# Triangular inverses of two linear-attention heads on 32-row diagonal blocks, with 32-column matmuls and block transposes on the vector engine

## The chip, the cores and the metric

One core of one Trainium2 chip runs the whole kernel in one launch. The metric is the device time in microseconds (us), the median of several executions. The kernel is written with a scheduling layer: the program is written in one order, and the layer lays down a fixed order of instructions for each engine, by data dependences, by free buffers and by priority (work written earlier goes first unless a `first()` block lifts it). Each engine then works through its own list in order.

## What is computed

The reference is three transformer blocks, one after the other, on 512 tokens of 1024 channels in float32. The change touches the second block alone, whose two mixers run on chunks of 128 tokens and need the inverse of a unit lower triangular matrix for each head and chunk:

```python
def chunk_gated_delta_rule(q, k, v, g, beta):        # "gdn" in the kernel
    ...
    lower = jnp.where(strict, jnp.einsum('bhncd,bhnsd->bhncs', k_beta, k) * decay, 0.0)
    t_mat = lax.linalg.triangular_solve(lower + eye, ..., left_side=True, lower=True, unit_diagonal=True)
    u = jnp.matmul(t_mat, v_beta)
    ...
def rwkv7_scan(r, decay, k, v, a, b):                # "rwkv" in the kernel, done chunk by chunk there
    def step(S, inp):
        sa = jnp.einsum('bhvk,bhk->bhv', S, a_t)
        S = S * w_t[...] + sa[..., None] * b_t[...] + v_t[..., None] * k_t[...]
        return S, jnp.einsum('bhvk,bhk->bhv', S, r_t)
```

Both mixers have 8 heads of 64 channels. A 128x128 inverse is needed for 4 chunks x 8 heads in each.

## The kernel before

Weights stream in pieces of eight 128x128 blocks (`load`, L318): a DMA, a copy to a high part on ACT (L325) and a subtraction for the low part on DVE (L326). A projection of 128 output columns (`lin`) is, for each of 8 weight blocks, three matmuls of 512 columns (L364, L365, L366): 24 in all. They are called weight matmuls below. Their results lie in three PSUM banks named `mm` and are read there by ACT and DVE.

The second block's mixers are in `second` (L1142). It runs over four columns of heads, j = 0 to 3, two heads a column. For each j, `rwkv` (L1297) and `gdn` (L1450) are generators that `run` steps in turn, so that their instructions are written alternately. Then come the projections for the next column (`lins(j + 1)`: seven of 24 weight matmuls) and one or two projections for gates (`aside`; twelve after the last column). Being written later, they have lower priority, and the scheduling layer puts their weight matmuls wherever it holds TensorE (PE) to be free. Tiles of `rwkv` have names with `ra` and PSUM banks `r` (3), those of `gdn` `ga` and `g` (2).

Each of the two calls `invert` (L677) once a head, so 4 inverses a column and 16 in all; one call does the four chunks together, in tiles of 128x512 (`Lt`: the strictly triangular matrices; `Tt`: the inverse, transposed; `Ti`: the inverse). The two inverses of a mixer are stepped in turn. The method doubles the size of inverted diagonal blocks: from blocks of b rows to 2b, the off-diagonal part is minus a product of inverse, triangular matrix and inverse.

- Start: two DVE operations on 128x512 (L684, L685), four PE transposes into PSUM and one ACT copy out (L652 and L656, by `transposes`).
- Five levels, b = 2, 4, 8, 16, 32. Each: an ACT copy that gathers the odd blocks of `Lt` (L700); a product of two 128x128 matmuls with 128 columns (L704); a mask on DVE out of PSUM (L708, 128x256); a second such product (L711); a subtraction on DVE (L713, 128x256); and, so that `Tt` follows `Ti`, an ACT copy that gathers (L692), two PE transposes and an ACT copy out of PSUM (`turned`, by L652 and L656). After b = 32 there are four transposes instead.
- End, from 64 to 128: four 64x64 matmuls (L724), DVE (L727), four more (L731), DVE (L733).

All are float32, and a float32 matmul stands in the trace as two records, a transpose as one.

Of the kernel before, what the change touches and what calls it, by code (L numbers as in the profile page):

```python
# [11 lines left out]
AF = mybir.ActivationFunctionType  # L12
ALU = mybir.AluOpType
# [4 lines left out]
P = 128  # L18
# [43 lines left out]
def prep(i, only=(1, 2, 3)):  # L62
# [85 lines left out]
    c.add("m1", ((r[None] % 2 == 1) & (r[:, None] == r[None] - 1)).astype(f))  # L148
    g = np.arange(64)
    for b in (2, 4, 8, 16, 32):  # L150
        c.add(f"lev{b}", (r[:, None] // b == r[None] // b).astype(f))
# [422 lines left out]
class Chain:  # L574
# [102 lines left out]
    def invert(self, Lt, out):  # L677

        z, V, A, T = self.z, self.z.V, self.z.A, self.z.T
        quad = lambda x: x.rearrange("p (u n) -> p u n", u=4)  # L680
        Tt, Ti = self.t(), self.t()
        out.append(Tt)
        bc = lambda x, n: x.unsqueeze(1).to_broadcast([P, 4, n])
# [4 lines left out]
        odd = lambda x, b: x.rearrange("p (g two b) -> p g two b", two=2, b=b)[:, :, 1, :]  # L688

        def turned(b):  # L690
            some = z.tile("m" + self.sb, 256)
            A.activation(some.rearrange("p (g b) -> p g b", b=b), odd(Ti, b), AF.Copy)  # L692
            self.transposes(some, Tt[:, :256], 2)


        for b in (2, 4, 8, 16, 32):
            half = Ti.rearrange("p (g two b) -> p g two b", two=2, b=b)[:, :, 0, :]
# [3 lines left out]
            if b == 2:  # L701
                turned(b)
            for u in range(2):
                T.matmul(ps[:, u * P:u * P + P].rearrange("p (g b) -> p g b", b=b), lhsT=low[:, u * P:u * P + P],  # L704
                         rhs=half[:, u * P // b:(u + 1) * P // b], start=True, stop=True)
            m = z.tile("m" + self.sb, 256)
            two = lambda x: x.rearrange("p (u n) -> p u n", u=2)
            V.tensor_tensor(two(m), two(ps[:, :256]), z.k(f"lev{b}").unsqueeze(1).to_broadcast([P, 2, P]), op=ALU.mult)  # L708
# [6 lines left out]
            if b == 32:  # L715
                self.transposes(Ti, Tt)
            else:
                turned(2 * b)
# [1397 lines left out]
```

## Time and profile before

| | |
|---|---|
| median of 3 runs | 3348.91 us (3346.21 to 3350.74) |
| the profiled execution's own time | 3353.45 us, 4.5 us above the median |
| its span in the profile | 3351.7 us; 1.75 us lie around it |
| mean granted TensorE clock | 0.991 of full speed |
| busy: PE, DVE, ACT, POOL | 3262.8 us (97%), 2235.9 (67%), 1495.0 (45%), 101.0 (3%) |
| the stretch of the second block's mixers | about 1040 to 1500 us from the span's start |

The page has one row for each engine's busy time over the span, the span in 40 slices, the chain of work that ended last, and groups of instructions by source line. PE counts as busy until a matmul's result has left it, and matmuls overlap, so two back-to-back records of 0.27 us can start 0.11 us apart. What a record costs the engine is the distance from its start to the next one's. The views used below are the sums over chosen stretches, the groups by line, and the instructions in order of time, in which equal neighbours are merged into one row.

### The profile page before, as it was taken

What the parts mean: (1) busy time and instruction counts of PE and PEld (TensorE: products, weight loads), DVE (VectorE), ACT (ScalarE), POOL (GpSimd) and SP (SyncE); (2) the same over time, 40 slices, a digit from 0 to 9 for tenths busy, and PEclk for the clock granted to TensorE, in tenths of its full rate; (3) what the DMA queues carried; (4) which work ended last, traced back from release to release, by engine and by line L of the source; (5) the groups of instructions that cost most, each with busy time, mean ns of one, the idle gap of its engine ahead of it and who ended that gap; (6) DMA issues with size and microseconds to landing.
All of it is one profiled execution on the core that took longest, in us unless ns stands there. A gap on an engine that the chain in (4) does not pass through costs nothing. (4 is left out here: it accounts for less than half of the span.)

```text
span 3351.7 us, 46572 instructions
## 1 busy us (share of the span) xinstructions
PE 3262.8 (97%) x18165; PEld 2724.7 (81%) x18165; DVE 2235.9 (67%) x3675; ACT 1495.0 (45%) x2491; POOL 101.0 (3%) x186
## 2 busy tenths in 40 slices
PE   7999999999999999999999999999999999999998
PEld 6778888888887887887888888888877777888887
DVE  5696645976577677666886558786677996454344
ACT  6443433432346656653432334555546765232221
POOL 0000000000000000000000000000000001000000
PEclk9999999999999999999999999999999999999999
DMA  4223233664332112215467323222227567323322
GB/s 133 68 67 97 94 123 101 217 193 158 105 104 75 51 44 76 68 50 176 127 184 242 95 82 128 73 78 92 80 79 236 173 198 244 120 99 95 100 94 76
DMA packets 128317, 393.22 MB, mean 117 GB/s; under 512 B 16056, under 2 KB 23480, under 8 KB 128096
## 3 DMA queue, kind: packets, MB, share of 16 engines
q1 hardware_dynamic: 113776, 346.82, 32.9%
q0 software_dynamic: 13168, 42.36, 3.6%
q8 instruction: 143, 2.34, 0.3%
q10 hardware_dynamic: 1152, 1.05, 0.1%
q14 instruction: 78, 0.64, 0.1%
HBM read 358.44 MB, written 31.74 MB: 116 GB/s over the span
## 5 line engine op out<-in xcount | busy, mean ns | idle before, releaser
L364 PE MATMUL mm<-h,wh 128*128 128x512 f32 x2400 | 947.2, 395 | 1.1 <-ACT t L945 0.7
L365 PE MATMUL mm<-h,wh 128*128 128x512 f32 x2400 | 947.7, 395 | 0.0
L366 PE MATMUL mm<-h,wl 128*128 128x512 f32 x2400 | 947.1, 395 | 0.0
L325 ACT ACTIVATE wh<-wr 128x1024 fp32r<-128x1024 f32 x464 | 490.7, 1059 | 971.2 <-PE mm L365 692.8
L326 DVE TENSOR_TENSOR wl<-wr,wh 128x1024 fp32r<-128x1024 f32 x464 | 567.8, 1225 | 473.8 <-ACT wh L325 468.1
L366 PEld LDWEIGHTS mm<-h,wl 128*128 128x128 f32 x2400 | 452.5, 189 | 97.3 <-issue 6.0
L364 PEld LDWEIGHTS mm<-h,wh 128*128 128x128 f32 x2400 | 452.4, 189 | 96.7 <-issue 5.3
L365 PEld LDWEIGHTS mm<-h,wh 128*128 128x128 f32 x2400 | 452.6, 189 | 96.1 <-issue 5.3
L364 PE MATMUL mm<-p,wh 128*128 128x512 f32 x599 | 233.5, 390 | 0.0
L365 PE MATMUL mm<-p,wh 128*128 128x512 f32 x599 | 233.3, 389 | 0.1
L366 PE MATMUL mm<-p,wl 128*128 128x512 f32 x599 | 233.1, 389 | 0.0
L350 PE MATMUL mm<-h,wh 128*128 128x256 f32 (+1 forms) x480 | 161.1, 347 | 14.2 <-DVE t L1927 5.5
L351 PE MATMUL mm<-h,wh 128*128 128x256 f32 (+1 forms) x480 | 161.6, 341 | 1.5 <-DVE h L566 1.5
L352 PE MATMUL mm<-h,wl 128*128 128x256 f32 (+1 forms) x480 | 159.6, 337 | 0.0
L301 DVE SCALAR_TENSOR_TENSOR ac<-wa,adas,ac 128x1024 f32<-128x1024 f32 x98 | 125.4, 1280 | 25.7 <-DMA wa<-wa 25.2
L365 PEld LDWEIGHTS mm<-p,wh 128*128 128x128 f32 x599 | 112.4, 188 | 24.2 <-DVE p L426 0.8
L366 PEld LDWEIGHTS mm<-p,wl 128*128 128x128 f32 x599 | 112.4, 188 | 23.3
L364 PEld LDWEIGHTS mm<-p,wh 128*128 128x128 f32 x599 | 112.5, 188 | 23.2
L350 PEld LDWEIGHTS mm<-h,wh 128*128 128x128 f32 x480 | 93.8, 200 | 25.8 <-ACT h L565 4.5
L351 PEld LDWEIGHTS mm<-h,wh 128*128 128x128 f32 x480 | 95.4, 200 | 10.6 <-DVE h L566 2.8
L352 PEld LDWEIGHTS mm<-h,wl 128*128 128x128 f32 x480 | 95.2, 199 | 8.7
L747 DVE SCALAR_TENSOR_TENSOR f<-mm,par,f 128x511 f32<-128x511 f32 (+1 forms) x128 | 95.4, 745 | 1.1
(661 smaller groups left out, 5290.3 us busy)
## 6 DMA issues: line engine op xcount, KB each, us to landing
wr<-w SPq DMA_DIRECT2D x464, 512.0 KB, 3.5
wa<-wa SPq DMA_DIRECT2D x96, 512.0 KB, 4.3
e<-cum SPq DMA_DIRECT2D x64, 256.0 KB, 5.3
x<-x POOLq DMA_DIRECT2D x40, 256.0 KB, 5.2
s<-ecum SPq DMA_DIRECT2D x64, 128.0 KB, 4.7
cd<-t POOLq DMA_DIRECT2D x24, 256.0 KB, 2.3
gt<-t POOLq DMA_DIRECT2D x16, 256.0 KB, 2.5
fr<-gt SPq DMA_DIRECT2D x16, 256.0 KB, 3.0
```

The source lines that it names most:

```text
L301: self.V.scalar_tensor_tensor(a, raw, s[:, k, m:m + 1], a, op0=ALU.mult, op1=ALU.add)
L325: self.A.activation(hi, raw, AF.Copy)
L326: self.V.tensor_tensor(lo, raw, hi.bitcast(F32), op=ALU.subtract)
L350: self.T.matmul(ps[:, n], lhsT=wh, rhs=x[0][k][:, n], start=k == 0, stop=False)
L351: self.T.matmul(ps[:, n], lhsT=wh, rhs=x[1][k][:, n], start=False, stop=False)
L352: self.T.matmul(ps[:, n], lhsT=wl, rhs=x[0][k][:, n], start=False, stop=k == last)
L364: self.T.matmul(out, lhsT=wh, rhs=x[0][k], start=k == 0, stop=False)
L365: self.T.matmul(out, lhsT=wh, rhs=x[1][k], start=False, stop=False)
L366: self.T.matmul(out, lhsT=wl, rhs=x[0][k], start=False, stop=k == last)
L747: z.V.scalar_tensor_tensor(out[:, d:], src[:, :S - d], w[:, n - 1 - d:n - d], out[:, d:], op0=ALU.mult, op1=ALU.add)
```

## The change

`invert` is rewritten; outside of it only its tables of constants differ and two tiles are added (`ira`, `iga`: 128x128, two each). The triangular matrix is cut into its 32x32 diagonal blocks. `Tc` (in `ira` or `iga`) holds the four diagonal blocks of each of the four chunks in 128x128; `Lb` and `Tt` hold them block-diagonally in 128x512. The helper `each` makes one product of 16 matmuls (4 chunks x 4 blocks): the stationary operand is 128 rows x 32 columns, and the moving one has 16 or 32 columns. Four levels (b = 2 to 16) use it twice each; one more step with two such products goes from blocks of 32 to 64; the end from 64 to 128 is as before. `Tt` follows by a DVE transpose (in 32x32 blocks) and four ACT copies of 32 partitions; no PE transpose is left in `invert`. The code after it stands 25 lines lower, the code ahead of it 3.

```diff
     def invert(self, Lt, out):
-        Tt, Ti = self.t(), self.t()
+        Tt, Lb = self.t(), self.t()
+        Tc, Ttc = z.tile("i" + self.sb, P), z.tile("m" + self.sb, P)
+        def each(ps, lhs, rhs):
+            for u in range(4):
+                for i in range(4):
+                    T.matmul(ps(rows[i], u), lhsT=lhs[:, u * P + 32 * i:u * P + 32 * i + 32], rhs=rhs(u),
+                             start=True, stop=True)
-        V.tensor_tensor(quad(Tt), quad(Lt), bc(z.k("m1"), P), op=ALU.mult)
-        V.tensor_tensor(quad(Tt), bc(z.ident, P), quad(Tt), op=ALU.subtract)
-        self.transposes(Tt, Ti)
+        V.tensor_tensor(quad(Lb), quad(Lt), bc(z.k("lev32")), op=ALU.mult)
+        for i in range(4):
+            A.activation(quad(Tc)[rows[i]], cut(Lt)[rows[i], :, i], AF.Copy)
+        V.tensor_tensor(quad(Ttc), quad(Tc), bc(z.k("m1")), op=ALU.mult)
+        V.tensor_tensor(quad(Ttc), bc(z.k("id32")), quad(Ttc), op=ALU.subtract)
+        for u in range(4):
+            V.tensor_tensor(cut(Tt)[:, u], ..., op=ALU.mult)
+        V.transpose(Tc, Ttc)
         yield
-        for b in (2, 4, 8, 16, 32):
-            low = z.tile("m" + self.sb, 256)
-            A.activation(low.rearrange("p (g b) -> p g b", b=b), odd(Lt, b), AF.Copy)
-            for u in range(2):
-                T.matmul(ps[:, u * P:u * P + P]..., lhsT=low[:, u * P:u * P + P], rhs=half[...], ...)
-            V.tensor_tensor(two(m), two(ps[:, :256]), z.k(f"lev{b}")..., op=ALU.mult)
+        for b in (2, 4, 8, 16):
+            each(lambda r, u: wide(ps[r, 16 * u:16 * u + 16]), Lb, lambda u: even[:, n * u:n * u + n])
+            m = z.tile("m" + self.sb, 64)
+            V.tensor_tensor(quad(m), quad(ps[:, :64]), bc(z.k(f"lev{b}")), op=ALU.mult)
             yield
-            for u in range(2):
-                T.matmul(ps[:, 256 + u * P:384 + u * P], lhsT=Tt[:, u * P:u * P + P], rhs=m[:, u * P:u * P + P], ...)
-            V.tensor_tensor(half, half, ps[:, 256:]..., op=ALU.subtract)
-            yield
-            turned(2 * b)     # for b = 32: self.transposes(Ti, Tt)
+            each(lambda r, u: ps[r, 64 + 16 * u:80 + 16 * u], Tt, lambda u: m[:, 16 * u:16 * u + 16])
+            V.tensor_tensor(even, even, wide(ps[:, 64:128]), op=ALU.subtract)
+            if b == 16:
+                V.tensor_tensor(quad(Lb), quad(Lt), bc(z.k("off32")), op=ALU.mult)
+            Ttc = z.tile("m" + self.sb, P)
+            V.transpose(Ttc, Tc)
+            for i in range(4):
+                A.activation(cut(Tt)[rows[i], :, i], quad(Ttc)[rows[i]], AF.Copy)
             yield
+        each(lambda r, u: ps[r, 32 * u:32 * u + 32], Lb, lambda u: Tc[:, 32 * u:32 * u + 32])
+        A.activation(m, ps[:, :P], AF.Copy)
+        yield
+        each(lambda r, u: ps[r, P + 32 * u:P + 32 * u + 32], Tt, lambda u: m[:, 32 * u:32 * u + 32])
+        A.activation(y[:, :P], ps[:, P:2 * P], AF.Copy, scale=-1.0)
+        V.transpose(y[:, P:], y[:, :P])
+        yield
+        V.memset(quad(first)[rows[0], :, 32:], 0.0)
+        ...                                  # five ACT copies of 32 partitions into first and Tt
```

Three places show what this does to the written order. The first is PE in the first column, in the middle of the inverses of both mixers (`r` is a PSUM bank of `rwkv`, `g` of `gdn`, `mm` a weight matmul). Before:

```order
L704 MATMUL r_8521<-ra_8279,mra_8522 128x128 x2
L366 MATMUL mm_9149<-h_4668,wl_9080 128x512
L652 MATMUL g_8537<-con_64,mga_8535 128x128 x2
L364 MATMUL mm_9149<-h_4670,wh_9079 128x512
L704 MATMUL r_8528<-ra_8289,mra_8529 128x128 x2
L652 MATMUL g_8543<-con_64,mga_8541 128x128 x2
L711 MATMUL r_8521<-mra_8526,ra_8278 128x128 x2
L711 MATMUL r_8528<-mra_8533,ra_8288 128x128 x2
```

The same place in the changed kernel:

```order
L696 MATMUL r_8714<-ira_8343,ra_8342 32x16 x16
L696 MATMUL r_8733<-ira_8359,ra_8358 32x16 x16
L696 MATMUL g_8676<-mga_8693,ga_8135 32x16 x16
L696 MATMUL g_8695<-mga_8712,ga_8202 32x16 x16
L696 MATMUL r_8714<-mra_8731,ra_8341 32x16 x16
L696 MATMUL r_8733<-mra_8750,ra_8357 32x16 x3
L369 MATMUL mm_9684<-h_4675,wl_9615 128x512
L696 MATMUL r_8733<-mra_8750,ra_8357 32x16 x13
```

A product of two wide matmuls has become one of 16 narrow ones, the transposes are gone, and the products of the two mixers still alternate with about one weight matmul to a round.

The second is DVE in the second column, where the inverses of `rwkv` start. Before:

```order
L684 TENSOR_TENSOR ra_9454<-ra_9413,con_64 128x512
L713 TENSOR_TENSOR ga_9313<-ga_9313,g_9415 128x128x2
L326 TENSOR_TENSOR wl_11218<-wr_11215,wh_11217 128x1024
L708 TENSOR_TENSOR mga_9439<-g_9428,con_64 128x256
L685 TENSOR_TENSOR ra_9454<-con_64,ra_9454 128x512
L713 TENSOR_TENSOR ga_9374<-ga_9374,g_9428 128x128x2
L684 TENSOR_TENSOR ra_9464<-ra_9446,con_64 128x512
L685 TENSOR_TENSOR ra_9464<-con_64,ra_9464 128x512
```

And in the changed kernel:

```order
L699 TENSOR_TENSOR ra_10054<-ra_9960,con_64 128x512
L723 STREAM_TRANSPOSE mga_10024<-iga_9849 128x128
L719 TENSOR_TENSOR iga_9916<-iga_9916,g_9981 128x32x2
L702 TENSOR_TENSOR mra_10056<-ira_10055,con_64 128x128
L723 STREAM_TRANSPOSE mga_10047<-iga_9916 128x128
L703 TENSOR_TENSOR mra_10056<-con_64,mra_10056 128x128
L702 TENSOR_TENSOR mra_10072<-ira_10071,con_64 128x128
L705 TENSOR_TENSOR ra_10053<-con_64,mra_10056 128x128 x4
L707 STREAM_TRANSPOSE ira_10055<-mra_10056 128x128
```

Two wide operations for the start of an inverse (L684, L685) have become eight (L699, L702, L703, four of L705, L707).

The third is ACT in the first column, at the place of the first. Before:

```order
L692 ACTIVATE mra_8503<-ra_8279 128x256
L700 ACTIVATE mga_8497<-ga_8186 128x256
L692 ACTIVATE mra_8509<-ra_8289 128x256
L656 ACTIVATE ra_8278<-r_8505 128x256
L700 ACTIVATE mra_8522<-ra_8237 128x256
L656 ACTIVATE ra_8288<-r_8511 128x256
```

And in the changed kernel:

```order
L725 ACTIVATE ga_8135<-mga_8601 32x4x32 x4
L725 ACTIVATE ga_8202<-mga_8624 32x4x32 x4
L725 ACTIVATE ra_8341<-mra_8647 32x4x32 x4
L725 ACTIVATE ra_8357<-mra_8670 32x4x32 x4
L725 ACTIVATE ga_8135<-mga_8770 32x4x32 x4
L725 ACTIVATE ga_8202<-mga_8794 32x4x32 x4
```

Three copies of 128x256 for a level have become four of 32 partitions x 128, and they come in runs of four for one inverse after another.

## Rows read from the trace of the kernel before

**Rows 1.** Sums over stretches (us from the span's start): the stretch and its length, then busy time and instructions of PE, PE's weight loads, DVE, ACT and POOL, then the granted TensorE clock (1.00 is 2.4 GHz, 0.50 is 1.2 GHz), the DMA share and GB/s. The first four are the parts of the second column of heads, the fifth is the whole of the four columns, the last two come after them.

```profile
1162.00:1199.00 37.00, 35.76 (x183) 29.46 (x182) 35.53 (x64) 20.84 (x39) 0.00 (x0) 1.00 0.28 90
1199.00:1214.00 15.00, 15.00 (x110) 13.36 (x111) 9.38 (x18) 7.52 (x18) 0.54 (x1) 1.00 0.17 54
1214.00:1249.00 35.00, 34.95 (x290) 31.93 (x289) 19.96 (x47) 21.80 (x56) 0.00 (x0) 1.00 0.05 16
1249.00:1280.00 31.00, 29.87 (x199) 24.33 (x198) 18.77 (x38) 21.24 (x30) 0.54 (x1) 1.00 0.08 26
1040.00:1500.00 460.00, 453.08 (x3039) 388.13 (x3038) 320.11 (x621) 278.78 (x540) 14.07 (x26) 1.00 0.19 60
1500.00:1560.00 60.00, 56.84 (x263) 46.54 (x262) 37.34 (x55) 26.89 (x33) 1.63 (x3) 0.94 0.47 148
...
1520.00:1540.00 20.00, 16.84 (x63) 13.35 (x62) 14.09 (x19) 5.92 (x9) 0.00 (x0) 0.83 0.52 168
```

**Rows 2.** Groups by line and shape on PE from 1040 to 1500 us: line, tiles, stationary rows*columns, moving operand, count of records, then busy us (overlaps counted once) and mean ns of one, idle time before. `g` rows are of `gdn`, `r` rows of `rwkv`.

```profile
L704 PE MATMUL g<-ga,mga 128*128 128x128 f32 x160 | 26.3, 283 | 0.0
L711 PE MATMUL g<-mga,ga 128*128 128x128 f32 x160 | 26.0, 285 | 0.0
L711 PE MATMUL r<-mra,ra 128*128 128x128 f32 x160 | 25.6, 286 | 0.0
L704 PE MATMUL r<-ra,mra 128*128 128x128 f32 x160 | 25.5, 281 | 0.1
L652 PE MATMUL g<-con,mga 128*128 128x128 f32 x80 | 16.3, 279 | 0.0
L652 PE MATMUL r<-con,mra 128*128 128x128 f32 x80 | 15.7, 278 | 0.1
L652 PE MATMUL r<-con,ra 128*128 128x128 f32 x96 | 14.1, 273 | 0.0
L652 PE MATMUL g<-con,ga 128*128 128x128 f32 x64 | 9.5, 273 | 0.0
L731 PE MATMUL r<-ra,mra 64*64 64x64 f32 x64 | 5.4, 224 | 0.0
L724 PE MATMUL r<-ra,ra 64*64 64x64 f32 x64 | 4.6, 221 | 0.0
```

**Rows 3.** PE's records in order of time, in the inverses of the first two columns: start (us), us from the first start to the last end, engine, line, tiles, shape, how many in a row.

```profile
1094.71 0.60 PE L704 MATMUL g<-ga,mga 128*128 128x128 f32 x4
1095.15 0.38 PE L652 MATMUL r<-con,mra 128*128 128x128 f32 x2
1095.37 1.24 PE L711 MATMUL g<-mga,ga 128*128 128x128 f32 x8
1096.45 0.61 PE L704 MATMUL r<-ra,mra 128*128 128x128 f32 x4
...
1105.03 1.14 PE L724 MATMUL g<-ga,ga 64*64 64x64 f32 x16
1106.10 0.50 PE L364 MATMUL mm<-h,wh 128*128 128x512 f32 x1
...
1210.34 0.71 PE L704 MATMUL g<-ga,mga 128*128 128x128 f32 x4
```

**Rows 4.** The same view in the third block (2143 to 2150 us), where another part of the kernel has narrow products: L1796 makes 16 matmuls with a stationary operand of 128 rows x 32 columns and 32 moving columns, into PSUM partitions 0, 32, 64 and 96 in turn, in the same form as `each`.

```profile
2146.62 0.39 PE L364 MATMUL mm<-h,wh 128*128 128x512 f32 x1
2146.84 0.39 PE L365 MATMUL mm<-h,wh 128*128 128x512 f32 x1
2147.16 0.46 PE L1796 MATMUL two<-a,a 128*32 128x32 f32 x32
2147.55 0.50 PE L366 MATMUL mm<-h,wl 128*128 128x512 f32 x1
2147.89 0.39 PE L364 MATMUL mm<-h,wh 128*128 128x512 f32 x1
```

**Rows 5.** Groups by line and shape on DVE, whole span: line, operation, tiles, out<-in, count, then busy us, mean ns of one, idle time before and what ended it.

```profile
L708 DVE TENSOR_TENSOR mra<-r,con 128x256 f32<-128x256 f32 x40 | 17.0, 425 | 26.9 <-PE r L704 20.6 <-ACT mga L700 4.0 <-ACT ga L656 1.9
L1479 DVE SCALAR_TENSOR_TENSOR ga<-g,q,ga 128x128 f32<-128x128 f32 x32 | 9.5, 342 | 0.6 <-PE g L1475 0.6
L539 DVE TENSOR_SCALAR f<-con,nw 128x128 f32<-128x128 f32 x32 | 8.3, 300 | 0.4
L1808 DVE TENSOR_TENSOR a<-a 32x64 f32<-32x64 f32 x32 | 6.9, 216 | 0.4
L684 DVE TENSOR_TENSOR ra<-ra,con 128x512 f32<-128x512 f32 x8 | 5.5, 685 | 0.0
```

**Rows 6.** DVE in order of time in the second column, the operation that reads what the last row of Rows 3 made.

```profile
1211.16 0.43 DVE L708 TENSOR_TENSOR mga<-g,con 128x256 f32<-128x256 f32 x1
```

**Rows 7.** Groups by line and shape on ACT, whole span, columns as in Rows 5.

```profile
L692 ACT ACTIVATE mra<-ra 128x256 f32<-128x256 f32 x40 | 16.8, 421 | 7.7 <-DVE ra L713 7.2
L656 ACT ACTIVATE ra<-r 128x256 f32<-128x256 f32 x40 | 15.5, 386 | 6.7 <-PE r L652 5.9
```

**Rows 8.** ACT in order of time in the second column: two copies of 128 columns in a row, and one of 32 partitions.

```profile
1168.26 0.49 ACT L1286 ACTIVATE lx<-lw 128x128 fp32r<-128x128 f32 x2
1168.76 0.31 ACT L1315 ACTIVATE lx<-lw 32x128 fp32r<-32x128 f32 x1
```

More of the change, by code (lines that the diff above doesn't have):

```diff
@@ L147, in prep @@
     c.add("strict", (r[None] > r[:, None]).astype(f))
[L148 to L151 removed]
+    l, g = r[:, None] % 32, np.arange(32)[None]
+    c.add("m1", ((g % 2 == 1) & (l == g - 1)).astype(f))
+    c.add("id32", (l == g).astype(f))
+    for b in (2, 4, 8, 16):
+        c.add(f"lev{b}", ((l // (2 * b) == g[:, :16] // b) & (l // b % 2 == 1)).astype(f))
+    c.add("lev32", (r[:, None] // 32 == r[None] // 32).astype(f))
+    c.add("off32", ((r[:, None] // 32 % 2 == 0) & (r[:, None] // 32 == r[None] // 32 - 1)).astype(f))
     c.add("rs128", np.broadcast_to((np.arange(S) % 128 != 0).astype(f), (P, S)))
@@ L680, in invert @@
         quad = lambda x: x.rearrange("p (u n) -> p u n", u=4)
-        Tt, Ti = self.t(), self.t()
+        cut = lambda x: x.rearrange("p (u i n) -> p u i n", u=4, i=4)
+        bc = lambda x: x.unsqueeze(1).to_broadcast([P, 4, x.shape[1]])
+        rows = [slice(32 * i, 32 * i + 32) for i in range(4)]
+        Tt, Lb = self.t(), self.t()
         out.append(Tt)
-        bc = lambda x, n: x.unsqueeze(1).to_broadcast([P, 4, n])
-        V.tensor_tensor(quad(Tt), quad(Lt), bc(z.k("m1"), P), op=ALU.mult)
@@ L685, in invert @@
-        V.tensor_tensor(quad(Tt), bc(z.ident, P), quad(Tt), op=ALU.subtract)
-        self.transposes(Tt, Ti)
-        yield
[L688 to L697, printed above, removed]
-            ps = self.bank()
-            low = z.tile("m" + self.sb, 256)
-            A.activation(low.rearrange("p (g b) -> p g b", b=b), odd(Lt, b), AF.Copy)
-            if b == 2:
-                turned(b)
-            for u in range(2):
[L704 to L708, printed above, removed]
-            yield
-            for u in range(2):
-                T.matmul(ps[:, 256 + u * P:384 + u * P], lhsT=Tt[:, u * P:u * P + P], rhs=m[:, u * P:u * P + P],
-                         start=True, stop=True)
-            V.tensor_tensor(half, half, ps[:, 256:].rearrange("p (g b) -> p g b", b=b), op=ALU.subtract)
-            yield
-            if b == 32:
-                self.transposes(Ti, Tt)
-            else:
-                turned(2 * b)
-            yield
@@ L722, in invert @@
+        first = z.tile("m" + self.sb, 256)
+        V.memset(quad(first)[rows[0], :, 32:], 0.0)
+        for r, src in ((rows[0], Tc), (rows[1], y[:, :P])):
+            A.activation(quad(first)[r, :, :32], quad(src)[r], AF.Copy)
+        A.activation(quad(first)[rows[1], :, 32:], quad(Tc)[rows[1]], AF.Copy)
+        for i in (0, 2):
+            A.activation(cut(Tt)[rows[i], :, i + 1], quad(y[:, P:])[rows[i + 1]], AF.Copy)
         ps = self.bank(256)
         for u in range(4):
-            T.matmul(ps[o, 64 * u:64 * u + 64], lhsT=Lt[e, u * P + 64:u * P + P], rhs=Ti[e, u * P:u * P + 64],
+            T.matmul(ps[o, 64 * u:64 * u + 64], lhsT=Lt[e, u * P + 64:u * P + P], rhs=first[e, 64 * u:64 * u + 64],
```

11 lines of the change are left out of this document (10 added, 1 removed).

## The prediction

> **What bounds the kernel now.** I read the sums over stretches first, then PE's groups by line, then PE's records in order of time, and DVE's and ACT's groups last. In the stretch that the change touches, 1040 to 1500 us, PE is busy 453.08 of 460 us at the full clock of 2.4 GHz, DVE 320.11 and ACT 278.78 [rows 1]. The reader is to see that the column of heads has parts with different company: in its first 37 us DVE is full too (35.53), in the 35 us where all four inverses run (call it the dense stretch) PE is full (34.95) and DVE and ACT are little over half busy [rows 1]. Busy alone is weak evidence, since a record counts 0.27 us and costs less. The records in order of time settle it: in the dense stretch they start one behind the other, 0.11 us apart, and the groups by line have almost no idle time ahead of them [rows 2, 3]. So PE's own work sets the length of the dense stretch, and work taken off PE there is time, until another chain takes over. Ahead of and behind this stretch the engines' written lists are the same, apart from shifts of a few weight matmuls, so I look for nothing elsewhere.
>
> **PE, work removed and added.** Counts per inverse are the records of rows 2 over 8 inverses a mixer.
> - L711: 20 records; eight of them take from 1095.37 to 1096.45, 0.135 us each [rows 3]: 2.70 us.
> - L704: 20 records at 0.11 (four from 1094.71 to 1095.15): 2.20 us.
> - Transposes in L652: 4 at the start, 10 in the levels, 4 at the end, 18 at 0.11 (two from 1095.15 to 1095.37): 1.98 us. Of the 96 records of `r<-con,ra` 64 are of the inverses.
> - The 64x64 products: 16 records; 16 take from 1105.03 to 1106.10, 0.067 each: 1.07 us. They stay.
>
> That is 7.95 us an inverse. Now the narrow products. The third block has the very form: 128 rows x 32 columns, output in four partition groups in turn; 16 matmuls (32 records) take from 2147.16 to 2147.55, 0.39 us, 0.012 a record [rows 4]. Ten such an inverse are 3.90 us, and with the 64x64 ones 4.97. PE saves 2.98 us an inverse, **48 us** for 16, if nothing else steps in.
>
> Bounds of the price: eight of the ten products move 16 columns instead of 32. If columns set the 0.39 us, they cost half, and PE saves 25 us more; I take 0.39, since the nearest row has it. A product behind a weight matmul starts 0.10 us late (0.32 instead of 0.22 us from 2146.84) [rows 4]; at most 16 us over all 160 products, but the old ones paid at such changes too. Upward the nearest row is the 64x64 record at 0.067 us; that case is a rival below.
>
> **DVE.** Before, an inverse has two operations of 512 columns at 0.685 and twelve of 256 columns at about 0.425 [rows 5]: 6.5 us. Afterwards: two of 512 (1.37), six of 128 at 0.30 (1.80), eight of 64 at 0.22 (1.76), two of 256 (0.85), a small memset (0.22), and six block transposes of 128x128, an operation that no row shows. Its bounds are 0.22 (the 64-column row) and 0.685 (four times the columns); I take 0.34, the dearer 128-column row [rows 5]. Sum 8.0 us, so 1.6 us more an inverse, 25 us in all. The Trainium skill, VectorE: DVE Perf Modes, section on the three transpose paths, gives 311 ns for a 128x128 transpose of two-byte elements on DVE; with it the sum would be 7.9.
>
> In the dense stretch this hides (DVE 19.96 of 35). Where the inverses start it may not: the start costs 0.685 + 6 x 0.30 + 0.34 = 2.8 us instead of 1.4, 1.4 more each, 5.8 a column, and DVE is full in the first 37 us. Two things stand against that: PE's list is shorter ahead of it by 3.5 us a column (the 11.9 saved less the 8.4 of the dense stretch, below), and from 1199 to 1214 DVE has 5.6 us free. Bounds for the part ahead of the dense stretch: -3.5 to +5.8 us a column; I take 0.
>
> **ACT.** Fifteen copies of 256 columns at 0.39 to 0.42 [rows 7] and two wider ones become 27 copies of 128 columns, at 0.245 (two in 0.49) to 0.31 [rows 8]: 6.6 to 8.4 us instead of over 6.1. ACT has 13 us free in the dense stretch, four inverses add at most 2.3 each: hidden as work, but the copies lie in the chain.
>
> **The dense stretch, new length.** PE's list of it holds, in the first two columns, about 31 products (12.1 us), 18 weight matmuls at 0.225 (4.1), 64 records of 64x64 (4.3), 42 other records of 128 columns (4.6) and some 15 changes of form (1.5): 26.6 us, against 35.
>
> Against that stands the chain of one mixer's pair. One level of one inverse: product to last result 0.46 [rows 4], mask 0.22, product 0.46, subtraction 0.22, transpose 0.34, four copies 1.05, and five handovers at 0.11 (a product ends at 1211.05, its reader starts at 1211.16) [rows 3, 6]: 3.3 us. The second inverse's copies queue on ACT behind the first's and the next product waits for them: 4.3 us a round. Four rounds are 17.2, the step from 32 to 64 about 4.3 (its two copies out of PSUM, a transpose and five copies), the end 3.0: 24.5 us. Work of 26.6 and a chain of 24.5 share one list that is taken in order, with hardly a weight matmul between, so they will not overlap fully. I take **29 us**, 6 less than now; 24 us over four columns.
>
> What is late next: after the dense stretch the solves follow on PE as before (29.87 of 31 us busy), so 6 us earlier there is 6 us earlier at the end. The 37 or so gate matmuls that move from behind the last column into it are 8 us of work moved, not saved. DMA is idle in the dense stretch (share 0.05) and no queue is moved past. Constants shrink by 384 columns and nothing waits for them.
>
> **Sum.** 3353.45 - 24 = 3329.5 us for the profiled execution, which stood 4.5 above the median: **3325 us**. The likeliest case's own range is a dense stretch of 26.6 to 32.5 us and the rest within 1.5 us a column: 3309 to 3339.
>
> **The rivals.**
> - *PE is the bound throughout.* Everything freed is filled: 48 us, 3301. For it: PE full in all parts now, and the lists hold weight matmuls before and after the dense stretch. Against: hardly any inside it.
> - *The cover is gone.* The chain with its waits is as long as the old PE work (a round of 7 us: 4 x 7.0 + 7.3 = 35); or the clock falls. In 1520 to 1540 us PE was busy 16.84 of 20 and the granted clock came to 0.83 [rows 1]; 26.6 us of PE work at 0.83 are 5.4 us more a column, 22 in all, and the gain is gone: 3347 to 3349. The Trainium skill, TensorEngine Tiling (Array Packing), section PSUM Bottleneck, warns that tiling speeds TensorE and leaves the copies out of PSUM, which may then set the pace; it is this rival's direction.
> - *The chain is longer than the old work.* PE takes products in written order, so a product that waits for its four copies holds up the other mixer's ready one. If the two mixers' levels run one after the other instead of beside each other, a round is twice a pair's 4.3, say 8 us, and the dense stretch 4 us longer than now; with 1.5 us a column from DVE at the starts, 22 us: 3371. It decides from 7 us a round on. For it: sixteen copies a round, in runs of four, are up to 5 us of ACT. Against: ACT needs 5 of those 7.
> - *Narrow records are dear in long runs.* The 32 records of rows 4 stand alone between weight matmuls; here 1,000 follow each other. At half the 64-column record's 0.067 us a product is 1.07 us, PE loses 61 us: 3410. Nothing is left from 0.69 us a product on. For it: no such run in the trace. Against: the run of 32 shows no sign of slowing.
>
> The Trainium skill, TensorE: Matmul & The Clock Gate, section on the 56 ns gap, says that two matmuls never start less than about 25 ns apart however few columns they move. By that rule, an estimate, a product is 0.80 us, the 48 us saved turn into 18 us lost, 3367. The trace disagrees: 0.012 us a record, so I give that rule no more than its place in the last rival.
>
> **How the numbers follow.** Forecast 0.55, PE throughout 0.12, cover gone 0.14, longer chain 0.10, dear records 0.09. A measurement of this kernel tells some 0.2%, 6.7 us, from no change: faster 0.67, same 0.14, slower 0.19. The range goes from the second case (3301) to the better part of the fourth (3362); outside lie the dear records, the worst chains and PE savings beyond 48 us, together under 2 in 10.
>
> **What would show it.** Right: L696 in runs with about 0.012 us a record; the dense stretch 26 to 32 us with PE below full and DVE or ACT ending its waits; the granted clock 1.00 in it; the first part of a column as long as now. Wrong: products of 0.6 us or more; a granted clock below 0.95 in the dense stretch; copies L725 above 0.31 us or transposes L723 above 0.5; a dense stretch of 34 us or more, or the first part 4 us longer, with PE waiting for DVE there.

## The result, and the profile after

| | before | after |
|---|---|---|
| median of the runs beside each other (us) | 3349.82 (3346.21 to 3355.05) | 3378.53 (3377.54 to 3388.13) |
| span of the profiled execution (us) | 3351.7 | 3376.0 |
| mean granted TensorE clock, whole span | 0.99 | 0.98 |
| PE records, whole span | 18165 | 22357 |

The ratio is 1.0092, 95% interval 1.0074 to 1.0109: the change costs 29 us, where 24 us were forecast to be won. DVE and ACT are busy 66% and 45% of the span, as before (67% and 45%).

The loss lies in the four columns of heads. I read the sums over stretches first. The first line is the second column's stretch from the last product ahead of the levels (L1413, L1388 of before) to the first of the score products that follow its solves (L1392, L1367); the dense stretch of [rows 1], 1214 to 1249 us in the kernel before, is the greater part of it there. The second line is all four columns. Columns as in [rows 1].

```profile
1223.00:1268.00 45.00, 37.79 (x1183) 31.16 (x1182) 21.13 (x76) 28.38 (x91) 0.00 (x0) 0.77 0.06 20
1022.00:1530.00 508.00, 469.77 (x7353) 378.22 (x7351) 334.21 (x816) 327.48 (x728) 15.92 (x29) 0.92 0.20 61
```

The same two stretches of the kernel before, in the same view:

```profile
1213.00:1255.00 42.00, 41.95 (x352) 38.39 (x351) 23.68 (x56) 23.59 (x59) 0.00 (x0) 1.00 0.04 14
1022.00:1499.00 477.00, 469.39 (x3112) 400.81 (x3110) 330.86 (x639) 294.26 (x564) 14.62 (x27) 1.00 0.19 60
```

Two things are new. PE has 7.2 us free in a stretch where it had none, and yet the stretch is 3 us longer; and the mean granted clock is 0.77: of its two levels PE had 1.2 GHz for some 20 of the 45 us. Next the groups by line on PE, 1040 to 1560 us, which answer to [rows 2] (last: idle time before, and what ended it):

```profile
L696 PE MATMUL r<-mra,ra 128*32 128x16 f32 x1024 | 22.1, 201 | 6.4 <-issue 6.4
L696 PE MATMUL r<-ira,ra 128*32 128x16 f32 x1024 | 17.6, 199 | 9.6 <-issue 8.3 <-ACT cra L1415 0.9 <-DVE ira L719 0.4
L696 PE MATMUL g<-mga,ga 128*32 128x16 f32 x1024 | 16.8, 193 | 6.3 <-issue 6.2
L696 PE MATMUL g<-iga,ga 128*32 128x16 f32 x1024 | 14.1, 187 | 4.1 <-issue 4.1
```

The idle time ahead of the narrow products is not put down to DVE or ACT but to `issue`: PE waited for nothing that the profile shows. The view of waits, PE alone, 1022 to 1530 us (us in total, times, longest), says the same; no later line reaches half of either of the first two:

```profile
PE r L696 <- issue: 14.7, 8, 2.5
PE g L696 <- issue: 13.1, 8, 2.1
PE r L616 <- ACT ra L1311: 5.9, 3, 2.6
PE g L749 <- ACT mga L743: 1.2, 3, 0.5
```

Sixteen waits for `issue`, 27.8 us. PE's records in order of time show what they have in common, and answer to [rows 3]:

```profile
1091.98 0.34 PE L696 MATMUL r<-mra,ra 128*32 128x16 f32 x19 [1.65 <-issue]
1092.14 0.19 PE L696 MATMUL g<-iga,ga 128*32 128x16 f32 x2
1092.16 0.19 PE L696 MATMUL r<-mra,ra 128*32 128x16 f32 x2
1092.17 0.81 PE L696 MATMUL g<-iga,ga 128*32 128x16 f32 x62
1092.85 0.54 PE L696 MATMUL r<-ira,ra 128*32 128x16 f32 x43
1095.81 0.46 PE L696 MATMUL r<-ira,ra 128*32 128x16 f32 x19 [2.42 <-issue]
...
1099.85 0.52 PE L696 MATMUL r<-mra,ra 128*32 128x16 f32 x24 [1.20 <-issue]
```

From one wait to the next there are 19 + 2 + 2 + 62 + 43 = 128 records, each with its weight load: 256 instructions. They run in some 1.4 us (1091.98 to 1093.4), and the next ones come 3.83 us after the first. The view of DMA from 1088 to 1100 us, in 40 slices of 0.3 us, has three packets of one queue and nothing else:

```profile
GB/s 0 0 0 0 0 55 0 0 0 0 0 0 0 0 0 0 0 55 0 0 0 0 0 0 0 0 0 0 0 0 0 0 55 0 0 0 0 0 0 0
...
q8 instruction: 3, 0.05, 1.8%
```

The packets lie at 1089.5, 1093.1 and 1097.6, and PE starts again at 1091.98, 1095.81 and 1099.85, each time 2.3 to 2.7 us later. That this queue carries PE's instructions can be counted: its line in the page of the change, and in that of the kernel before, is

```profile
q8 instruction: 176, 2.88, 0.4%
q8 instruction: 143, 2.34, 0.3%
```

A packet is 16 KB. PE's records and as many weight loads, 256 to a packet, would be 175 packets in the change and 142 before. So the theory after the first reading, **T1**: PE runs out of instructions. A product is 32 records of 0.011 us (62 records from 1092.17 to 1092.85), and they run out faster than the next packet of 256 instructions comes. The rivals: **T2**, the chain of transposes and copies sets the dense stretch and the waits are its shadow; **T3**, the clock falls because narrow products keep so little moving in PE, whether it waits or not (in T1 alone the waits would be what lowers it).

DVE's and ACT's groups, 1040 to 1540 us, answer to [rows 5, 7, 8]: the block transpose and the four copies behind it.

```profile
L723 DVE STREAM_TRANSPOSE mra<-ira 128x128 f32<-128x128 f32 x32 | 9.0, 294 | 0.6
L707 DVE STREAM_TRANSPOSE iga<-mga 128x128 f32<-128x128 f32 x8 | 2.5, 307 | 0.0
L719 DVE TENSOR_TENSOR ira<-ira,r 128x64 f32<-128x64 f32 x32 | 6.5, 204 | 21.4 <-PE r L696 21.4
L725 ACT ACTIVATE ra<-mra 32x128 f32<-32x128 f32 x128 | 39.5, 308 | 11.8 <-DVE mra L723 8.9
L725 ACT ACTIVATE ga<-mga 32x128 f32<-32x128 f32 x128 | 39.5, 308 | 21.3 <-DVE mga L723 12.4 <-PE r L696 5.6 <-PE g L696 0.3
```

### The profile page after: what moved, and what is told of

Its sections match the earlier page's. It is cut to its first block, busy times and chain, and to the rows that moved or that the text cites. A ratio compares the mean times of both kernels' runs of the same rounds, so it can differ in the third digit from the quotient of the medians.

```text
span 3376.0 us, 55288 instructions
## 1 busy us (share of the span) xinstructions
PE 3248.4 (96%) x22357; PEld 2689.6 (80%) x22357; DVE 2237.5 (66%) x3851; ACT 1524.4 (45%) x2649; POOL 101.2 (3%) x186
## 4 chain that ended last, share of the span: by engine, by line
PE 50%; DVE 4%; ACT 2%; DMA 1%; issue 1%; SPq 0%; DVEq 0%; ACTq 0%
PE mm L367 11%; PE mm L368 11%; PE mm L369 11%; PE mm L353 2%; PE mm L354 2%; PE mm L355 2%; PE s L2104 1%; DVE wl L329 1%; PE s L2090 1%; PE s L2058 1%; DMA e<-cum 1%; ACT wh L328 1%; PE aux L311 0%; PE mm L404 0%; PE s L2048 0%
```

## The experiments

The times are medians, each beside runs of the kernel before on the same chip (medians of 3347 to 3350 us); ratios are to before. A table gathers what I added up from the records: over the four columns, from the first record of L1345 to the last of the score products behind the fourth column's solves (L1392; the same source lines in each kernel), each record's time to the next record's start, by kind. The 512-column records are the weight matmuls and, in each kernel, 78 of the mixers' own. "Other" holds old products, transposes, 64x64 and the mixers' other matmuls. A wait here is a narrow record whose successor starts over 0.6 us later, so its count and time differ a little from those of the views, which hold idle time alone.

| kernel | stretch, us | 512 columns: records, us | other, us | narrow: records, us | waits: number, us |
|---|---|---|---|---|---|
| before | 476.2 | 933, 239.1 | 237.1 | none | none |
| after | 508.0 | 986, 270.4 | 137.0 | 5120, 100.5 | 18, 32.3 |
| added | 561.9 | 925, 237.2 | 262.7 | 5120, 62.1 | none |
| bunched | 579.2 | 902, 231.6 | 264.5 | 5120, 83.1 | 18, 31.8 |
| onepass | 480.2 | 992, 282.5 | 146.1 | 2560, 51.6 | 4, 4.5 |
| onepass_short | 436.7 | 964, 257.1 | 140.1 | 2560, 39.5 | 7, 8.1 |
| before_top | 450.8 | 993, 258.4 | 192.3 | none | none |
| mixed_r | 482.7 | 964, 251.6 | 188.1 | 2560, 43.0 | 5, 5.5 |

Under each run is its line of the sums over this stretch (columns as in [rows 1]).

### Is it the number of instructions?

**four** and **eight.** In `each`, sixteen matmuls become four (or eight of 64 columns):

```diff
-                for i in range(4):
-                    T.matmul(ps(rows[i], u), lhsT=lhs[:, u * P + 32 * i:u * P + 32 * i + 32], rhs=rhs(u),
+                T.matmul(ps(slice(0, P), u), lhsT=lhs[:, u * P:u * P + P], rhs=rhs(u), start=True, stop=True)
```

> Every narrow product is four matmuls of a 128-column stationary block instead of sixteen of 32 columns (the blocks off the diagonal are zero, so the sum is the same); DVE, ACT and all waits between engines stay as in the change. T1 (PE gets its instructions too slowly: 32 records with 32 weight loads a product, issue gaps of 2 us): the gaps ahead of the products go, the granted clock in the dense stretches returns to 1.00, time 3300 to 3335 us, below both kernels. T2 (the chain of DVE transposes and ACT copies sets the dense stretch): the chain is as long as in the change, time 3368 to 3385. T3 (products of 16 columns leave the array so idle that the clock falls, whatever the issue): gaps go, half clock in the dense stretches stays, time 3355 to 3375.

> Eight matmuls of 64 columns a product, half the instructions of the change, all else as in the change. T1: fewer than half the issue gaps, low clock shorter, time between the change and the kernel with four, 3320 to 3355 us. T2: 3368 to 3385. T3: clock as in the change, 3360 to 3380.

Measured: four 3550.59 us, ratio 1.0614 (1.0598 to 1.0630); eight 3423.47, ratio 1.0229 (1.0193 to 1.0264). All three theories missed. Of four, the sums and the records in order of time:

```profile
1022.00:1697.00 675.00, 656.01 (x3522) 576.21 (x3520) 337.80 (x816) 330.17 (x731) 15.66 (x29) 0.78 0.14 45
```

```profile
1092.70 1.91 PE L695 MATMUL g<-iga,ga 128*128 128x16 f32 x16
1094.46 0.31 PE L655 MATMUL r<-con,ra 128*128 128x128 f32 x1
...
1099.13 1.87 PE L695 MATMUL g<-iga,ga 128*128 128x16 f32 x8
1100.84 1.87 PE L695 MATMUL r<-ira,ra 128*128 128x16 f32 x8
```

And of eight, in the same two views:

```profile
1022.00:1587.00 565.00, 551.13 (x4795) 450.50 (x4795) 337.05 (x815) 327.25 (x727) 15.11 (x28) 0.85 0.17 54
```

```profile
1088.28 1.11 PE L696 MATMUL g<-iga,ga 128*64 128x16 f32 x32
1089.32 0.33 PE L655 MATMUL r<-con,ra 128*128 128x128 f32 x1
```

PE has no wait for `issue` left in either, as T1 said. But a record with a stationary operand of 128 columns takes 0.11 us though it moves only 16 columns (1.76 us for 16 from 1092.70), as long as one that moves 128, and 0.21 us at the lower clock (1.71 us for 8 from 1099.13); with 64 columns it is 0.033 us (32 from 1088.28 to 1089.32). So the fewer, wider products are dearer in themselves, and these kernels do not price the supply. They do tell on the clock: in four it is 0.78 without one such wait. Waits for instructions are not needed for it to fall, which is what T3 claims against T1.

**twice.** Each narrow matmul of the change issued twice (`for i in list(range(4)) * 2`).

> The change with every narrow matmul issued twice, 32 a product. T1 (supply): PE's narrow lines grow by as much again as they now take from start to start, about 100 us (0.63 us a product, 160 products): 3440 to 3490 us, twice as many issue gaps. T2 (chain): what is added is 0.2 us a product back to back (0.006 us a record), 36 us at most and partly inside waits: 3385 to 3415. T3: more records mean less idle array, the clock does not fall further: 3385 to 3415.

Measured: 3485.37, ratio 1.0419 (1.0394 to 1.0444), 107 us above the change; T1's range, and far over the 36 us that the expectation gave to back-to-back records. The waits, 1040 to 1540 us:

```profile
PE r L696 <- issue: 37.0, 25, 2.3
...
PE g L696 <- issue: 29.8, 18, 2.4
```

43 waits where the change has 16, and 58, of 90.6 us, up to the end of this kernel's four columns (1637 us): the waits grow with the instructions in a row, while DVE's and ACT's work is the same.

**added** and **bunched.** The kernel before, with as many narrow matmuls as the change has, doing nothing useful; once spread (16 ahead of each product), once in two bunches of 80 an inverse:

```diff
+            for _ in range(5 if b in (2, 16) else 0):      # bunched; added: once, ahead of each product
+                for u in range(4):
+                    for i in range(4):
+                        T.matmul(ps[32 * i:32 * i + 32, 16 * u:16 * u + 16], lhsT=low[:, 32 * i:32 * i + 32],
+                                 rhs=low[:, 16 * u:16 * u + 16], start=True, stop=True)
```

> The kernel before with sixteen narrow matmuls (32 columns stationary, 16 moving) put ahead of each of the ten products of an inverse, into the bank that the product then writes; DVE, ACT and the chain are those of the kernel before. T1: issue gaps of about 2 us appear among the added records and the granted clock falls below 1.00 in the dense stretches; 160 times up to 0.63 us, 3410 to 3460 us. T2: nothing in the chain got longer, no gaps; 160 times 0.2 to 0.39 us, 3380 to 3412, at a clock of 1.00. T3: the array is as busy as before or busier around them, so the clock stays at 1.00: 3380 to 3412.

> The kernel before with as many added narrow matmuls as in the run that put sixteen ahead of each product (which was 89 us slower, with no issue gap and a clock of 0.99), but in two bunches of eighty an inverse, ahead of the first products of levels 2 and 16. T1: bunches of the two mixers follow each other, 160 records and more in a row, the supply falls behind: at least 25 issue gaps of over 1 us, up to 3.9 us for 128 records, 3440 to 3500 us. If the supply is no limit and what cost there was the change of form between records: 5120 records at 0.0087 us are 45 us, 3385 to 3410, no gaps. Granted clock: by T3 and by T1 alike below 0.99, since PE moves few columns in a bunch whether it waits or not.

Measured: added 3435.83, ratio 1.0265 (1.0248 to 1.0282); bunched 3452.04, ratio 1.0301 (1.0285 to 1.0316). Added:

```profile
1022.00:1583.00 561.00, 552.74 (x8213) 464.12 (x8214) 330.87 (x637) 293.45 (x564) 14.56 (x27) 0.99 0.17 52
```

Bunched, the sums and its narrow groups from 1040 to 1540 us:

```profile
1021.00:1600.00 579.00, 535.95 (x8196) 459.99 (x8195) 330.12 (x637) 298.58 (x566) 14.18 (x26) 0.96 0.16 49
```

```profile
L706 PE MATMUL g<-mga 128*32 128x16 f32 x2240 | 25.0, 189 | 10.6 <-issue 10.3
L706 PE MATMUL r<-mra 128*32 128x16 f32 x1988 | 20.9, 186 | 10.9 <-issue 10.9
```

This is the cleanest pair: same records, same chain, other arrangement. Spread, 160 products take 62.1 us, 0.39 us each, and there is no wait; this is the price that the prediction had from [rows 4]. Bunched, there are 18 waits of 31.8 us, the same as in the change (the expectation by T1 had at least 25; its time, 3440 to 3500, came). The time of added, 3436, fits T1's number, but not for T1's reason: 62 us are the products, and 26 the old matmuls around them (262.7 against 237.1 us), another 0.16 us for each product put between them. The clock stays at 0.99 in added and falls to 0.96 in bunched, less than in the change (0.92) with the same waits: the waits alone do not set it. Bunching lengthened the runs of narrow records together with the waits, so which of the two took it from 0.99 to 0.96 is not shown.

**onepass.** The products read the upper halves of the operands as bfloat16, so that each matmul is one record:

```diff
+        top = lambda x: x.bitcast(BF16).rearrange("p (n h) -> p n h", h=2)[:, :, 1]
-                    T.matmul(ps(rows[i], u), lhsT=lhs[:, u * P + 32 * i:u * P + 32 * i + 32], rhs=rhs(u),
+                    T.matmul(ps(rows[i], u), lhsT=top(lhs)[:, u * P + 32 * i:u * P + 32 * i + 32], rhs=rhs(u),
```

> The change, with the narrow products fed by the upper sixteen bits of each operand (a view as bfloat16), so that each matmul is one record and one weight load instead of two; the lower bits are left out of these products. DVE, ACT and every wait stay as they are. T1 (supply: in the change 128 records with their 128 weight loads come every 3.9 us while PE waits for nothing the profile shows): half the instructions, under 15 of the 40 issue gaps, 3325 to 3350 us. T2 (chain of transposes and copies): 3365 to 3380, gaps replaced by waits for DVE and ACT. T3 (the clock falls because few columns move): still fewer columns, the granted clock in the dense stretches as low or lower than in the change, 3350 to 3380.

Measured: 3350.48, ratio 0.9998 (0.9988 to 1.0007): 28 us below the change, with 4 waits left of 18.

```profile
1023.00:1503.00 480.00, 464.26 (x4798) 359.14 (x4797) 332.75 (x816) 327.63 (x730) 15.61 (x29) 0.90 0.20 64
```

The time is where T1's range ends and T3's begins. The narrow products fell by 49 us, but the clock is at 0.90 with most of the waits gone, T3's sign, and the other records took back 21 of it. T1's own sign came only in part: the 40 gaps that the expectation counts are those of the weight loads (41 in the change, 38.8 us); 33 are left here, where under 15 were expected, though of 13.5 us. The view of waits from 1040 to 1540 us has a new first line for PE's weight loads:

```profile
PEld L697 <- ACT ra L726: 15.5, 38, 1.3
PEld L697 <- issue: 13.5, 33, 1.8
...
PEld L697 <- ACT ga L726: 11.4, 39, 1.6
```

L726 are the four copies behind the transpose. With the supply relieved, T2's chain comes up. The 28 us are no measure of the supply alone, since half of the records is also less work (before_top, below).

### What comes behind it

**shortcopy** and **onepass_short.** Three of the four copies are left out, in the change and in onepass: `for i in range(1)` at L725 and L726. What these two compute is no longer the inverse.

> The change with one of the four copies behind each level's transpose (the other three row groups of Tt keep what the start wrote, which is left out of the inverse): three ACT copies of 0.31 us fewer per level and inverse, 0.9 us off each step of the chain, PE's list as in the change. T2 (the chain sets the dense stretch): 4 levels x 0.9 us x two inverses in turn, some 4 to 7 us a column, 3350 to 3362 us. T1 with T3 (instruction supply and the low clock set it): the 16 gaps of 1 to 2.6 us and the half clock stay, 3370 to 3382.

> The kernel with single-record products (upper sixteen bits) and, as in the run beside it, one copy of four behind each level's transpose. There PE's weight loads waited 27 us for these copies. If the chain is what is next after the supply: 3325 to 3342 us. If the low clock is: the gaps close, but PE works at 1.2 GHz in the dense stretches, 3342 to 3352.

Measured: shortcopy 3373.44, ratio 1.0079 (1.0062 to 1.0095); onepass_short 3310.89, ratio 0.9887 (0.9872 to 0.9902). Shortcopy's waits on PE, 1040 to 1540 us, and its sums:

```profile
PE r L696 <- issue: 18.5, 11, 2.2
PE g L696 <- issue: 15.7, 9, 2.3
```

```profile
1023.00:1522.00 499.00, 458.05 (x7326) 377.55 (x7325) 332.54 (x815) 260.84 (x532) 15.16 (x28) 0.90 0.19 60
```

Onepass_short:

```profile
1022.00:1459.00 437.00, 422.07 (x4772) 338.07 (x4771) 329.06 (x815) 261.90 (x535) 15.45 (x28) 0.95 0.21 68
```

The same cut is worth 5 us while instructions are short (the two intervals overlap, so it may be nothing) and 40 us when they are not; in shortcopy PE's waits for `issue` grew from 27.8 to 34.2 us instead. That is what two limits in a row look like: the first hides the second. (onepass_short came out below what either theory had.)

**onepass_split** and **onepass_mask.** The whole computation of onepass, with a shorter way from transpose to product: two copies on ACT and two on DVE beside them, or one DVE operation for all four.

```diff
-            for i in range(4):
+            for i in range(2):
                 A.activation(cut(Tt)[rows[i], :, i], quad(Ttc)[rows[i]], AF.Copy)
+                V.tensor_copy(cut(Tt)[rows[i + 2], :, i + 2], quad(Ttc)[rows[i + 2]])
```

> Single-record products as before in this series, all four copies behind each level's transpose, two on ACT and two on DVE beside each other: 0.6 us of ACT less per level and inverse, some 0.4 us of DVE more. If ACT's run of four copies is the second limit: about two thirds of what leaving three out gave (40 us), 3318 to 3332 us. If it is any handover behind the transpose, or DVE takes what ACT gave: 3340 to 3352.

> Single-record products, and one DVE operation of 512 columns (0.685 us in its row) in place of the four ACT copies (1.23 us) and of one handover to ACT. If the chain is the second limit: 0.55 us and a handover off each step, 3320 to 3335 us. If DVE becomes the one that is waited for (21 of 47 us busy in a dense stretch, 11 us more): 3340 to 3355.

Measured: onepass_split 3331.25, ratio 0.9951 (0.9934 to 0.9968); onepass_mask 3338.36, ratio 0.9970 (0.9959 to 0.9981). Split:

```profile
1022.00:1483.00 461.00, 437.36 (x4801) 347.30 (x4800) 360.78 (x945) 293.28 (x604) 15.66 (x29) 0.93 0.20 66
```

Mask, with PE's longest wait ahead of a narrow product in the same stretch:

```profile
1022.00:1495.00 473.00, 443.63 (x4801) 351.28 (x4799) 366.69 (x881) 251.85 (x474) 15.63 (x29) 0.92 0.20 64
```

```profile
PE g L697 <- DVE mga L717: 3.5, 1, 3.5
```

Splitting ACT's run of four copies gives 19 of the 40 us, within the range that was expected if this run is the second limit. Mask lies between its two ranges. There the waits of the narrow products are for DVE, where the masks (L717) stand in the same list as the new operation, but the one shown is a single wait of 3.5 us: what holds mask 7 us above split is not shown.

**before_top.** The old products with the same upper halves.

> The kernel before with the upper sixteen bits in its ten products an inverse: 20 + 20 records become 10 + 10 an inverse. If PE's work bounds the dense stretches as the prediction said of the kernel before: half of 4.90 us an inverse, 39 us for 16, 3305 to 3320 us, and the single record alone is worth more in the old form than in the new. If waits take it back: 3325 to 3350.

Measured: 3321.54, ratio 0.9920 (0.9901 to 0.9940).

```profile
1022.00:1472.00 450.00, 437.21 (x2842) 353.65 (x2842) 327.47 (x639) 299.37 (x572) 15.61 (x29) 1.00 0.20 67
```

27 us are won, 1.5 us short of the range. It supports that PE's work bounded the dense stretch of before (shorter products also shorten the chain, which this run does not separate), and it is a control: the half of the records, not the narrow form, is what made onepass_split faster than before, and it is worth as much in the old form (27 us) as in the new (28). Both these kernels beat before and after, at the price of the lower bits in these products; of the two the old form is the better.

### The clock, and half of the change

**filled.** A matmul of 384 columns (256 for the last two) ahead of each narrow product, its output never read:

```diff
+            T.matmul(ps[:, 128:512].rearrange("p (c n) -> p c n", c=3), lhsT=z.onesr,
+                     rhs=z.bd64r.unsqueeze(1).to_broadcast([P, 3, P]), start=True, stop=True)
             each(lambda r, u: wide(ps[r, 16 * u:16 * u + 16]), Lb, lambda u: even[:, n * u:n * u + n])
```

> The change with one matmul of 384 columns (256 for the last two) in one pass ahead of each narrow product, its output never read: 0.17 us each, 27 us of PE work added, and little to fetch. T1 with the clock as a consequence of the gaps: the gaps shrink by the fillers but do not vanish, the granted clock stays below 0.99 where they remain, 3385 to 3405 us. T3: the moved columns hold the clock at 1.00 in the dense stretches, what the low clock cost comes back, 3355 to 3385. T2: the fillers lie in the waits of the chain, 3375 to 3385 at any clock.

Measured: 3377.43, ratio 1.0077 (1.0062 to 1.0092), the time of the change.

```profile
1023.00:1528.00 505.00, 488.34 (x7424) 387.60 (x7425) 335.20 (x812) 321.56 (x722) 13.81 (x26) 0.96 0.18 56
```

The fillers cost more than priced: from start to start 0.36 us each, 58 us in all, and yet the time did not grow: the narrow products took 80.3 us instead of 100.5, and 85 weight matmuls fewer lie in the stretch. The clock rose from 0.92 to 0.96 and the waits shrank (12, 11.1 us). The number fits T2 and T3 both and misses T1's. Part of the clock came back, as T3 said, but the waits shrank with it, so this run does not tell the two apart.

**mixed_r**, **mixed_g** and **onepass_r.** Narrow inverses in one mixer alone (`invert` chooses by the mixer's name), and mixed_r with single records.

> The inverses of the r mixer as in the change, those of the g mixer as in the kernel before (one of the masks of the old levels as a broadcast of eight columns, for room). T1: the narrow products of r come with old products between them, half as many instructions in the dense stretch: under 10 issue gaps, clock 1.00, half of the 48 us that PE should save, 3320 to 3340 us, faster than both kernels. T2: r's chain is as long as in the change and holds up the list: 3350 to 3370. T3: enough columns move, clock 1.00, as T1.

> The mirror of the run with narrow inverses in r alone: those of the g mixer as in the change, those of r as before. If what ate r's saving there (31 us of PE work fewer, 0 to 5 us slower) lies in narrow products as such (entry, exit, supply: 0.24 us over the back-to-back time each), the same here: 3345 to 3360. If it lies in the order (r's solve comes earlier, g's inverses follow it): g is now the short one, the dense stretch is as long as r's old chain, and 3330 to 3345 is possible.

> Narrow inverses in r alone, as single records (upper sixteen bits), g as before. Supply is no limit here and the columns that g moves hold the clock at 1.00, so what is left is work and chain. T1 and T3: 20 to 30 us of PE work fewer than before and nothing against it, 3318 to 3340 us, below both kernels. T2 (chains and order): 3342 to 3355.

Measured: mixed_r 3355.14, ratio 1.0015 (1.0006 to 1.0025); mixed_g 3355.42, ratio 1.0019 (1.0010 to 1.0028); onepass_r 3358.09, ratio 1.0030 (1.0021 to 1.0040). mixed_r:

```profile
1022.00:1504.00 482.00, 462.84 (x5195) 381.00 (x5194) 330.09 (x718) 308.15 (x642) 14.97 (x28) 0.99 0.19 62
```

The clock is back, 0.99, as T1 and T3 said, but the time lies in T2's range. In mixed_r the other matmuls fell by 49.0 us and the narrow ones took 43.0 of them, 0.54 us a product, though only 5.5 us lie in waits over 0.6 us; the stretch also holds 31 weight matmuls more than before (7.0 us). mixed_g did not come out ahead either and lies in the range for "narrow products as such", so the order of r and g is not the reason. But its narrow products took only 34.4 us, 0.43 us each, with one wait, so their price is not the whole reason either. onepass_r lies above both of its ranges: half the records won nothing there. What holds up a kernel in which the two mixers have levels of different length is not settled by these runs.

## Why the prediction was wrong

- **What bounds the kernel before: right as far as shown.** Old products with half the records (before_top) gave 27 us of the 39 that PE's work alone would give.
- **The price of a narrow product: right alone, wrong in a row; this is the step that failed.** 0.39 us was the price of 32 records between weight matmuls [rows 4], and added has it to the hundredth. In the change 160 products took 100.5 us, 0.63 us each, 38 us over the forecast's 62.4; that is beyond the 0.6 us named as the sign of error. Eighteen waits hold 32.3 us of it: PE waited for its own instructions, which the price left out. The other 6 are the clock: without the waits 1670 narrow records started at 1.2 GHz and took 0.016 us each, 3432 at 2.4 GHz and took 0.012, which is 0.39 us a product again. So all that left PE (100.1 us of other records, old products and transposes) came back as narrow products (100.5).
- **The granted clock of 1.00 in the dense stretch: wrong.** It was 0.77. At 1.2 GHz a weight matmul takes 0.43 us (1109.51 to 1109.94) where [rows 4] have 0.22, and the dense stretch now has many of them between its narrow products:

```profile
1109.51 0.63 PE L367 MATMUL mm<-h,wh 128*128 128x512 f32 x1
1109.94 0.63 PE L368 MATMUL mm<-h,wh 128*128 128x512 f32 x1
```

  The 512-column records of the four columns took 31.3 us more; 53 more weight matmuls, at 0.227 us, are 12.0, and most of the other 19 is the clock: 56 weight matmuls started at 1.2 GHz and took 0.54 us each to the next start, the other 852 took 0.25, which makes 16 us. The prediction had the fall of the clock in a rival, at 5.4 us a column; it came together with the supply.
- **The sum.** +100.5 narrow, -100.1 other, +31.3 the 512-column records: +31.7, the stretch's 31.8. Behind it 7.3 us come back, since weight matmuls moved ahead: 24.3 us, the difference of the spans. From the forecast to this: its 48 us of PE work saved were nothing (38 us dearer narrow products, 10 us fewer removed), 48 us; the dearer 512-column records 19; the moved weight matmuls 5 (12.0 less the 7.3); and the 24 us that it had set aside for the chain did not come on top: with most of the copies left out shortcopy won at most 5. -24 + 48 + 19 + 5 - 24 = +24. The last two terms are what the others leave, not measured by themselves. From the last product ahead of the levels to the end of the fourth inverse the four columns took 41 to 44 us, 36 to 38 before: 3 to 7 us longer, where 6 shorter were forecast. (A slip in the prediction: by its own terms, 32.5 us and 1.5 us a column, its likeliest case reaches up to 3345 and not 3339. Nothing rests on it.)
- **The chain of 24.5 us: probably too short, though not what decided.** It counted one mixer's pair, and both mixers' copies stand in ACT's one list. With three copies fewer the four dense stretches, from the last product ahead of the levels to the score products, were 28 to 33 us long instead of 40 to 42 (onepass_short against onepass), 10 us less on average; one pair's copies, 24 of 0.308 us, are 7.4. DVE and ACT themselves were priced well: the transpose 0.29 to 0.31 us (0.34 taken), the copy 0.308 (0.245 to 0.31).
- **The rivals.** "Narrow records are dear in long runs" was the right place with the wrong mechanism: not the record, which is as cheap as priced, but the instructions that have not come; its point of no gain, 0.69 us a product, was nearly reached (0.63), and the clock did the rest. The rule weighed there, that two matmuls never start less than about 25 ns apart (the Trainium skill, TensorE: Matmul & The Clock Gate, section on the 56 ns gap), does not hold for these records, which start 0.011 us apart; by it a product would take 0.80 us wherever it stands, where added shows 0.39 and the change 0.63. That its 3367 us lies nearer to the result than the forecast does is no support for it.

A sign that could have warned was in reach: the first table of the page counts instructions, and a product went from 4 records to 32. But PE has no wait for `issue` in these columns of the kernel before, so the rate at which instructions come could not be read there. The Trainium skill, Runtime: NRT & Kernel Launch, section Instruction fetch mechanics, has the blocks of 256 instructions that the trace shows, and holds that fetching them is hidden because an engine issues more slowly than they come. Here PE ran 256 in about 1.4 us and started the next ones 3.83 us after the first of them, so the measurement decides against the second half. Why a packet does not come earlier no run here shows.

## What to carry to other kernels

Price a small instruction in a run as long as the one that will be issued, and count the instructions as well as the time: here a block of 256 on PE (128 records with their loads) ran in 1.4 us while the next was ready only 3.8 to 4.0 us after the last, and in a row of such blocks PE waited for its own instructions. Between wider matmuls (added) the same records met no such wait. Such a wait is called `issue` in the views; look there before blaming the chain. And where one limit hides another, take away each by itself and both together (at most 5, 28 and 68 us here) before saying what the second is worth.

## What the hardware showed that was not expected

- While PE was out of instructions (1088 to 1100 us), they came in packets of 16 KB 3.6 and 4.5 us apart, and PE started again every 3.8 to 4.0 us.
- A float32 record's time from start to start, at 2.4 GHz, went with the columns of its stationary operand and not with the 16 it moved: 0.011 us (32 columns, four column groups in turn), 0.033 us (64, two groups in turn), 0.11 us (128).
- PE at 97% busy of a stretch was granted 0.78 of the clock with products that move 16 columns a record (four: 656.01 of 675 us), and at 98% it was granted 1.00 with products of 128 (before: 469.39 of 477). A busy PE is no sign of the full clock.
